# The gate's two VectorE operations at the ends of their units, and a pair of transposes side by side, in the attention loop of an encoder layer

## The chip, the cores and the metric

The kernel runs on one core of one Trainium2 chip. The metric is the device time of one launch in microseconds (us); the median of three runs stands for the kernel. A profile of one execution gives, for each engine, when each instruction ran: TensorE (PE, with its weight loads as PEld), VectorE (DVE), ScalarE (ACT), GpSimd (POOL) and SyncE (SP), which issues most of the transfers.

## The reference, cut to what matters

One encoder layer on two sequences of 512 rows and 1024 columns. An S5 state-space branch and a windowed attention branch (16 query heads, 4 key heads, windows of three blocks of 128) are merged under two gates; an output projection and a squared-ReLU MLP follow.

```python
h = rms_norm(x, ln1)
q, k, v, u, g_att, g_ssm = jnp.split(h @ w_in, IN_SPLITS, axis=-1)
...
s = einsum('nqkgd,njkd->nkgqj', qb, kw) * scale + bias      # banded, masked
p = softmax(concatenate([s, sink_col], -1), -1)[..., :-1]
y_att = einsum('nkgqj,njkd->nqkgd', p, vw)
...
y_ssm = y * sigmoid(y @ w_glu + b_glu)
mixed = sigmoid(g_att) * y_att + sigmoid(g_ssm) * y_ssm
x = x + mixed @ w_out
x = x + square(relu(rms_norm(x, ln2) @ w_up)) @ w_down
```

The change concerns `sigmoid(g_att) * y_att` (the gate's product), the softmax's division, which the kernel does on the finished head outputs, and the transposes of `p`.

## The kernel before, in words

Nearly every product of two matrices is made of three: each operand is split into a rounded high part (a copy on ScalarE) and the remainder, the low part (a subtraction on VectorE or GpSimd).

**The attention loop** (lines 1026 to 1131) runs over eight steps, one for each key head `j` and sequence `sq`. A step has four units, one for each block of 128 queries (`qb`, 0 to 3). A unit handles four heads against two key blocks (at the ends of the sequence) or three. The engines' order inside the loop is written out by hand for TensorE, ScalarE, VectorE and GpSimd (line 1026); SP is not in that list, and its order is the planner's.

Three units are in flight at any time. For the unit `cur`, TensorE computes the scores (`scores`, line 860, two `sps` banks in turn), VectorE adds the bias and takes the maximum (`largest`, line 866), ScalarE takes the exponential (`exp`). For the unit before, `prev`, TensorE transposes `p` block by block (`turn`, line 877, two `tps` banks in turn), ScalarE copies the high part (`high`), VectorE the low part (`low`), and TensorE multiplies by the values into the single bank `po` (`value`, line 892). ScalarE then copies the lower half of `po` (`lower_part`). For the unit before that, `owed`, VectorE adds the two halves into `ya` (`add`, line 902), which empties `po`; the first `value` of `prev` waits for it. Between all this, `project` feeds TensorE with the query projection of the next step (in step 7, which has no next step, with GLU products by `glu_pull`), followed by `square`, `power` (a sum of squares on VectorE and a power on GpSimd), `norm`, and the query's own `turn`, `high` and `low`.

**The gate and the division** of step i come during step i + 1, in the object `late` (class `Divide`, line 908). In block 1 the sums are inverted, transposed and sent through DRAM to be spread over the partitions (`fac`, line 931); the gate's tile is loaded (`load_gate`, line 934). In block 2 `gated` (line 939) multiplies `ya` by the gate. In block 3 `multiply` (line 943) multiplies `ya` by `fac` and stores the result to `mix_scr`. `fac` and the gate's tile take turns in the two buffers of the pool `evp`, tag `ev`. The bias tiles of the next key head are loaded by SP at the end of block 3 of every second step (line 1130).

**The tail** (lines 1132 to 1161) finishes the last unit, with GLU products between the transposes, and starts the merge. `load_gates` (line 688) loads `gs` and `at` (the finished attention from `mix_scr`) for one column of the merge, on GpSimd's queue; `at` uses the pool `evp`, tag `ev` as well. `lower` is the low part of the last piece of GLU weights, on GpSimd. `gated_states`, `mixed` and `parts_of` are the merge itself, mostly on VectorE.

Of the kernel before, what the change touches and what calls it, by code (L numbers as in the profile page):

```python
# [63 lines left out]
def hybrid_layer(ctx, tc, x, rel, onehot, w_qkv, w_ug, vectors, lam, coefs, w_glu, w_out, ln2,  # L64
# [15 lines left out]
    def acc():  # L80
        return ps_acc.tile([P, 512], F32, tag="acc", name="acc")
# [606 lines left out]
    def load_gates(m):  # L688
        tiles = [p.tile([P, NTOK], F32, tag=tag, name=name) for p, tag, name in
                 ((wq, "c_hi", "ga"), (wq, "c_lo", "gs"), (evp, "ev", "at"))]  # L690
        glu_in[m] = tiles
        for t_, scr in zip(tiles[1:], (gs_scr, mix_scr)):
            GP.dma_start(t_, scr[m])
# [32 lines left out]
    def mixed(u):  # L726
        m, s, (ga, gs, at) = sides(u)
        V.tensor_mul(ga, ga, gs)
        V.tensor_add(ga, ga, at)
# [6 lines left out]
    with tc.tile_pool(name="att", bufs=2, reuse_waits="tile") as ap, tc.tile_pool(name="attc", bufs=1, reuse_waits="tile") as ac:  # L736
# [63 lines left out]
        class Tile:  # L800
# [6 lines left out]
            def project(self, n):  # L807
                (j, sq), col = self.key, self.t * P
                for i in range(self.k, min(self.k + n, 3 * KT)):
                    k, p = divmod(i, 3)  # L810
                    hi, lo = weights[j][k // 4]
                    act, w = [(0, hi), (0, lo), (1, hi)][p]
                    PE.matmul(self.ps, hT[sq][act][:, k, col:col + P], w[:, k % 4, :], start=i == 0, stop=i == 3 * KT - 1)  # L813
                self.k += n
# [134 lines left out]
        def load_y(m):  # L949
            if m % 4 == 0:  # L950
                yT.append([q.rearrange("p (m s) k -> p m (s k)", s=2) for q in slot((slot_b, slot_a)[m // 4])])
            for e in range(2):
                SP.dma_start(yT[-1][e][:, m % 4, :].bitcast(F32), y2_scr[e, m * 8:(m + 1) * 8].rearrange("g c t k -> (g c) (t k)"))
# [15 lines left out]
        def glu_pull(n):  # L969
            for _ in itertools.islice(early, n):  # L970
                pass
# [39 lines left out]
        def pieces_of(i):  # L1011

            if i == 0:
                return weight_pieces(1)
            if i == 6:
                return glu_pieces(0, wq, GP)
            if i == 7:
                return glu_pieces(1, cpool, GP) + glu_pieces(2, cpool, GP)
            if i % 2 == 1:
                pending[:] = weight_pieces(i // 2 + 2) if i // 2 + 2 < N_KV else []  # L1020
                return pending[:2]
            return pending[2:]

        pending = []
        prev = owed = lower = None
        with tc.manual_schedule(engines={ET.PE, ET.Activation, ET.DVE, ET.Pool}):
            for i, (j, sq) in enumerate(steps):
                nxt = steps[i + 1] if i + 1 < len(steps) else None
                sums = small.tile([P, G, NB], F32, tag="sm", name="sm", bufs=2)
                ya = ap.tile([P, 2, HALF], F32, tag="ya", name="ya")  # L1030
                extra = pieces_of(i)
                for qb in range(NB):
                    if 1 <= i < 5:
                        e, t = divmod((i - 1) * NB + qb, T)
                        GP.dma_start(y2_scr[e, :, :, t, :].rearrange("g c k -> c g k"), y_scr[e, t])
                    for m in {6: (qb,), 7: ((4, 5), (6,), (7,), ())[qb]}.get(i, ()):
                        load_y(m)
                    cur = Unit(j, sq, qb, sums, ya)
                    n3 = prev.nkb if prev else 0
                    div = Divide(*steps[i - 1], *done) if qb == 1 and i > 0 else None  # L1040
                    new = Tile(*nxt, qb) if nxt else None
                    project = new.project if new else lambda n: glu_pull(n // 2)
                    kd = None
                    if rows and not nxt:
                        rows.pt = acc()
                    if rows and not rows.qn:
                        rows.power()
                    cur.scores(0)
                    cur.largest(0)
                    if qb == 2 and late:  # L1050
                        late.gated()
                    if qb == 3 and late:
                        late.multiply()
                    if i == 7 and qb == 3:
                        load_gates(0)
                        final = Divide(j, sq, sums, ya, True)
                        final.load_gate(ap, "p", 3)
                    cur.scores(1)
                    if owed:
                        owed.add()  # L1060
                    cur.largest(1)
                    if n3:
                        prev.turn(0)
                        prev.high(0)
                    project(6)
                    if n3:
                        prev.low(0)
                    cur.exp(0)
                    cur.exp(1)
                    if rows and not rows.qn:  # L1070
                        rows.norm()
                    if qb == 0 and nxt:
                        kd = key_copies(*nxt)
                    if div:
                        div.invert()
                    cur.scores(2)
                    cur.largest(2)
                    if n3:
                        prev.turn(1)
                        prev.high(1)  # L1080
                    project(4)
                    if n3:
                        prev.value(0, 0)
                    project(2)
                    cur.exp(2)
                    cur.scores(3)
                    if lower:
                        lower()
                        lower = None
                    if n3:  # L1090
                        prev.low(1)
                        prev.value(0, 1)
                    cur.largest(3)
                    if rows:
                        rows.turn()
                    if n3 > 2:
                        prev.turn(2)
                    if kd:
                        key_turn(*nxt, kd)
                    if div:  # L1100
                        div.turn()
                    project(4)
                    if rows:
                        rows.high()
                        rows.low()
                    if n3 > 2:
                        prev.high(2)
                    if n3:
                        prev.value(1, 0)
                    cur.exp(3)  # L1110
                    if n3 > 2:
                        prev.low(2)
                    project(4)
                    if n3:
                        prev.value(1, 1)
                    project(4)
                    if n3 > 2:
                        prev.value(2, 0)
                        prev.value(2, 1)
                    if new:  # L1120
                        new.square()
                    if n3:
                        prev.lower_part()
                    if extra:
                        lower = extra.pop(0)()
                    if qb == 1:
                        late = div
                    owed, prev, rows = prev, cur, new
                    if nxt and qb == NB - 1 and sq == 1:
                        load_biases(nxt[0])  # L1130
                done = sums, ya
            owed.add()
            glu_pull(6)
            for k in range(prev.nkb):
                prev.turn(k)
                prev.high(k)
                prev.low(k)
                glu_pull(4)
            lower()
            gate_out(0)  # L1140
            for k in range(prev.nkb):
                prev.value(k, 0)
                prev.value(k, 1)
            load_gates(1)
            prev.lower_part()
            prev.add()
            glu_pull(10)
            gate_out(1)
            final.invert()
            final.turn()  # L1150
            glu_pull(24)
            final.gated()
            for u in range(2):
                gated_states(u, ap, "qn")
                mixed(u)
            gate_out(2)
            gate_out(3)
            gated_states(2, ap, "qn")
            column_half(3, 0)
            column_half(3, 1)  # L1160
            final.multiply()
# [429 lines left out]
```

## Time and profile before

| | us |
|---|---|
| median of three runs | 1502.4 |
| lowest and highest of them | 1500.92, 1504.12 |
| the profiled execution | 1503.71 |
| its span, first to last instruction | 1501.9 |
| TensorE busy in it | 1453.4 |
| VectorE busy in it | 1106.8 |
| attention loop, from the first score product to the last exponential's unit | about 459.9 to 695 |

The span is that of the instructions; the execution's own time is 1.8 us longer. An entry of the timeline gives the start in us from the span's start, the length, the engine, the line of the kernel, the operation with its output and inputs, and in brackets how long the engine had been idle and what released it. The granted clock of TensorE is 0.998 of full speed over the span. Ends of matrix products are modelled in the profile, so a TensorE that is shown busy may still be short of its best rate.

### The profile page before, as it was taken

Reading aid. Unit: us, or ns where it says so; the run is one execution under the profiler, and the core shown is the slowest. Engines: PE = TensorE matmul, PEld = TensorE weight load, DVE = VectorE, ACT = ScalarE, POOL = GpSimd, SP = SyncE. Lnnn points to the kernel's source line nnn. Section 1 sums busy time; section 2 is a strip of 40 time slices with the busy share of each in tenths; the row PEclk is TensorE's granted clock in tenths of the full one; section 3 lists DMA queues with packets and bytes.
Section 4 is the critical chain, followed back from the end, with each engine's and each line's share of the span. In section 5 each row is a group of like instructions: output and inputs, shape, how many; then the busy total and the mean of one; then the engine's idle time right before and its main releaser. Section 6 shows DMA issues by size and latency. Waiting matters only on the chain.

```text
span 1501.9 us, 22138 instructions
## 1 busy us (share of the span) xinstructions
PE 1453.4 (97%) x8074; PEld 1230.0 (82%) x8074; DVE 1106.8 (74%) x1989; ACT 761.7 (51%) x1362; POOL 212.6 (14%) x372
## 2 busy tenths in 40 slices
PE   6999999999999999999999989999999999999998
PEld 4888888888999888887787868888888888888787
DVE  7998859976646888887975478777777588575653
ACT  6777852235536777775334254445555443433332
POOL 3133341002232443222100000000000000000000
PEclk9999999999999999999999999999999999999999
DMA  4455469229731445275544234444443794454441
GB/s 174 140 169 168 160 208 345 107 100 344 287 132 36 155 135 183 88 252 170 185 135 162 92 115 159 155 154 154 155 154 126 267 352 132 153 182 154 126 123 60
DMA packets 103165, 249.69 MB, mean 166 GB/s; under 512 B 12266, under 2 KB 23786, under 8 KB 103056
## 3 DMA queue, kind: packets, MB, share of 16 engines
q1 hardware_dynamic: 60528, 140.07, 28.7%
q0 software_dynamic: 16896, 53.53, 10.3%
q10 hardware_dynamic: 25632, 54.67, 9.7%
q8 instruction: 64, 1.05, 0.3%
q14 instruction: 45, 0.37, 0.1%
HBM read 173.74 MB, written 90.21 MB: 176 GB/s over the span
## 4 chain that ended last, share of the span: by engine, by line
PE 78%; DVE 8%; ACT 4%; DMA 4%; issue 3%; POOL 1%; ACTq 0%; SPq 0%; DVEq 0%; POOLq 0%
PE acc L185 14%; PE bank L117 13%; PE bank L118 13%; PE bank L116 13%; PE acc L813 4%; PE acc L123 3%; PE acc L117 2%; PE acc L118 2%; PE acc L116 2%; PE sps L547 2%; PE po L896 2%; PE sps L864 1%; PE tps L880 1%; PE sps L645 1%; DMA fac<-rs_scr 1%
## 5 line engine op out<-in xcount | busy, mean ns | idle before, releaser
L185 PE MATMUL acc<-act,c_hi 128*128 128x512 f32 x768 | 249.6, 400 | 1.0 <-DVE act L304 1.0
L117 PE MATMUL bank<-b_lo,a_hi 128*128 128x512 f32 x448 | 174.6, 390 | 1.6 <-DVE b_lo L1460 1.6
L118 PE MATMUL bank<-b_hi,a_lo 128*128 128x512 f32 x448 | 174.3, 389 | 0.0
L116 PE MATMUL bank<-b_hi,a_hi 128*128 128x512 f32 x448 | 173.5, 389 | 0.0
L185 PEld LDWEIGHTS acc<-act,c_hi 128*128 128x128 f32 x768 | 142.2, 189 | 29.1 <-DVE act L304 2.4
L185 PE MATMUL acc<-act,c_lo 128*128 128x512 f32 x384 | 152.5, 397 | 0.0
L1459 ACT CAST a_hi<-d_a 128x1024 fp32r<-128x1024 f32 x56 | 59.0, 1054 | 179.7 <-PE bank L117 176.4
L116 PE MATMUL bank<-act,act 128*128 128x512 f32 x368 | 144.1, 391 | 4.9 <-ACT act L1349 4.9
L117 PE MATMUL bank<-act,act 128*128 128x512 f32 x368 | 143.7, 391 | 0.0
L118 PE MATMUL bank<-act,act 128*128 128x512 f32 x368 | 143.7, 391 | 0.0
L1460 DVE TENSOR_TENSOR a_lo<-d_a,a_hi 128x1024 fp32r<-128x1024 f32 x56 | 68.5, 1224 | 99.9 <-ACT a_hi L1459 99.9
L813 PE MATMUL acc<-w_hi,act 128*128 128x256 f32 x512 | 116.2, 295 | 0.0
L117 PEld LDWEIGHTS bank<-b_lo,a_hi 128*128 128x128 f32 x448 | 84.1, 188 | 20.1 <-DVE b_lo L1460 2.6
L116 PEld LDWEIGHTS bank<-b_hi,a_hi 128*128 128x128 f32 x448 | 84.1, 188 | 17.5
L118 PEld LDWEIGHTS bank<-b_hi,a_lo 128*128 128x128 f32 x448 | 84.1, 188 | 17.3
L813 PEld LDWEIGHTS acc<-w_hi,act 128*128 128x128 f32 x512 | 87.0, 189 | 3.7
L874 ACT ACTIVATE p<-p,nmx 128x257 f32<-128x257 f32 (+1 forms) x128 | 72.1, 563 | 31.2 <-DVE nmx L868 30.2
L116 PEld LDWEIGHTS bank<-act,act 128*128 128x128 f32 x368 | 69.4, 189 | 19.7 <-ACT act L1349 5.3
L123 PE MATMUL acc<-act,gc_hi 128*128 128x512 f32 x256 | 82.6, 401 | 1.8 <-ACT gc_hi L683 1.8
L185 PEld LDWEIGHTS acc<-act,c_lo 128*128 128x128 f32 x384 | 72.4, 189 | 14.0 <-DVE c_lo L176 0.5
L118 PEld LDWEIGHTS bank<-act,act 128*128 128x128 f32 x368 | 69.4, 189 | 14.9 <-DVE act L1350 0.4
L117 PEld LDWEIGHTS bank<-act,act 128*128 128x128 f32 x368 | 69.5, 189 | 14.3
(328 smaller groups left out, 3434.4 us busy)
## 6 DMA issues: line engine op xcount, KB each, us to landing
d_a<-a_scr SPq DMA_DIRECT2D x56, 512.0 KB, 3.6
u_raw<-in_w_up_dram SPq DMA_DIRECT2D x32, 512.0 KB, 5.1
a_scr<-t ACTq DMA_DIRECT2D x64, 256.0 KB, 4.8
k<-in_w_down_dram SPq DMA_DIRECT2D x32, 512.0 KB, 6.4
c_raw<-in_w_ug_dram SPq DMA_DIRECT2D x48, 256.0 KB, 3.7
a_scr<-a ACTq DMA_DIRECT2D x46, 256.0 KB, 2.1
ct_scr<-ctab POOLq DMA_DIRECT2D x16, 576.0 KB, 3.7
ctab_in<-ct_scr POOLq DMA_DIRECT2D x16, 576.0 KB, 7.6
```

The costliest lines, as they stand in the source:

```text
L116: PE.matmul(ps, a[0], b[0], start=first, stop=False)
L117: PE.matmul(ps, a[0], b[1], start=False, stop=False)
L118: PE.matmul(ps, a[1], b[0], start=False, stop=last)
L123: PE.matmul(ps, w[wi][:, k, :], rows[yi], start=k + p == 0, stop=k == KT - 1 and p == 2)
L185: PE.matmul(ps, w[wi][:, k, :], hT[s][hi][:, k, :], start=n == 0, stop=n == 3 * KT - 1)
L547: PE.matmul(ps[:, i * P:(i + 1) * P], bm[:, ri, g, :], u_sb[:, gp * SH + g, :], start=True, stop=True)
L645: PE.matmul(o, ctab[:, g0 % SI + g, ri, 0:T * CH], st[:, ri, g].rearrange("p s k -> p (s k)"), start=False, stop=ri == 1)
L813: PE.matmul(self.ps, hT[sq][act][:, k, col:col + P], w[:, k % 4, :], start=i == 0, stop=i == 3 * KT - 1)
L874: S.activation(p, p, AF.Exp, bias=self.nmx[:, h:h + 1], scale=-1.0, accum_out=self.sums[:, h, self.qb:self.qb + 1])
L896: PE.matmul(self.po, vv, self.hl[i][part], start=i + part == 0, stop=i == self.nkb - 1 and part == 1)
L1459: S.copy(hi, src)
L1460: V.tensor_sub(lo, src, hi.bitcast(F32))
```

## The change

Four edits in the order written out by hand; no operation is added or taken away.

- `gated` leaves its place between the first and the second maximum of block 2, and is written behind the query projection's `square`, ahead of `lower_part`, at the end of the same block.
- `multiply` moves in the same way inside block 3, in steps 1 to 6. With it goes its store on SP.
- In step 7, `multiply` and `load_gates(0)` leave block 3 and stand in the tail, behind the last unit's transposes, high and low parts, and ahead of `lower` and `gate_out(0)`.
- The second block's four transposes, `prev.turn(1)`, move from behind the third head's scores to directly behind the first block's. Their copy, `prev.high(1)`, stays.

```diff
                     cur.scores(0)
                     cur.largest(0)
-                    if qb == 2 and late:
-                        late.gated()
-                    if qb == 3 and late:
-                        late.multiply()
                     if i == 7 and qb == 3:
-                        load_gates(0)
                         final = Divide(j, sq, sums, ya, True)
                         final.load_gate(ap, "p", 3)
                     cur.scores(1)
...
                     cur.largest(1)
                     if n3:
                         prev.turn(0)
+                        prev.turn(1)
                         prev.high(0)
                     project(6)
...
                     cur.scores(2)
                     cur.largest(2)
                     if n3:
-                        prev.turn(1)
                         prev.high(1)
                     project(4)
...
                     if new:
                         new.square()
+                    if qb == 2 and late:
+                        late.gated()
+                    if qb == 3 and late and nxt:
+                        late.multiply()
                     if n3:
                         prev.lower_part()
...
                 prev.high(k)
                 prev.low(k)
                 glu_pull(4)
+            late.multiply()
+            load_gates(0)
             lower()
             gate_out(0)
```

## The prediction

> **What bounds the kernel now.** I read the page's engine line first, then windows cut at the first score product of each unit (one query block of one step), then the timelines of VectorE and TensorE inside those windows, then the chain of waits. Steps are numbered 0 to 7, blocks 0 to 3; times are us.
>
> ```profile
> PE 1453.4 (97%) x8074; PEld 1230.0 (82%) x8074; DVE 1106.8 (74%) x1989; ACT 761.7 (51%) x1362; POOL 212.6 (14%) x372
> ```
>
> TensorE is busy 97% of the span, so an edit on another engine counts only where TensorE waits. The windows show where that is. In order: step 0 blocks 2 and 3 (no gate work there), step 1 blocks 2 and 3, step 2 block 0, step 4 block 3. Columns: length, then busy time (count) of TensorE, its weight loads, VectorE, ScalarE, GpSimd; clock; DMA share and GB/s.
>
> ```profile
> 471.68:479.41 7.73, 7.70 (x57) 7.01 (x56) 6.51 (x17) 6.61 (x16) 2.67 (x4) 1.00 0.12 37
> 479.41:486.34 6.93, 6.93 (x56) 6.61 (x55) 5.77 (x16) 5.69 (x15) 3.54 (x5) 1.00 0.32 91
> 499.48:508.35 8.87, 8.33 (x56) 7.07 (x55) 7.97 (x19) 6.63 (x17) 3.63 (x5) 1.00 0.62 196
> 508.35:516.14 7.79, 7.67 (x56) 6.72 (x54) 6.83 (x18) 5.28 (x14) 2.27 (x4) 1.00 0.88 293
> 516.14:522.64 6.50, 6.50 (x53) 6.26 (x52) 5.39 (x16) 5.05 (x13) 2.85 (x5) 1.00 0.35 118
> 597.67:606.38 8.71, 7.65 (x55) 6.72 (x54) 6.89 (x18) 5.28 (x14) 1.43 (x3) 1.00 0.40 141
> ```
>
> Step 0 does the same matrix work without a gate: block 2 takes 7.73 there and 8.87 in step 1, block 3 takes 6.93 and 7.79. VectorE's timeline, a piece of the chain of waits, and TensorE's timeline (steps 1 and 7) say why.
>
> ```profile
> 501.03 1.23 DVE L941 TENSOR_TENSOR ya<-ya,gate 128x1024 f32<-128x1024 f32 x1
> 502.18 0.84 DVE L906 TENSOR_TENSOR ya<-po,ol 64x256 f32<-64x256 f32 x2
> ```
> ```profile
> 501.11 1.15 DVE ya L941
> ```
> ```profile
> 503.16 0.47 PE L896 MATMUL po<-ph,va 128*128 128x512 f32 x1 [0.39 <-DVE ya L906]
> ...
> 682.23 0.47 PE L896 MATMUL po<-ph,va 128*128 128x512 f32 x1 [1.00 <-DVE ya L906]
> ...
> 691.21 0.47 PE L896 MATMUL po<-ph,va 128*128 128x512 f32 x1 [1.80 <-DVE ya L906]
> ```
>
> The first value product needs the one `po` bank, which VectorE's `add` (L906) empties. The gate's product (L941) stands ahead of that `add` and lies on the chain with its full 1.15 (its row says 1.23; what follows starts 0.08 before its end). In block 3 the division (L945, 1.22 to 1.23, so some 1.14 on a chain) stands at the same place. That is the wait the change removes; the count of operations stays.
>
> **The change, part by part.**
>
> *Product out of block 2 (steps 1 to 6).* Step 0's block 2 has the same number of TensorE entries but one and the same ScalarE time (6.61 against 6.63), so I take its length: 8.87 - 7.73 = 1.14 less, six times.
>
> *Division out of block 3.* By step 0, 7.79 - 6.93 = 0.86. It delayed VectorE by 1.14 and cost 0.86, so a block forgives 1.14 - 0.86 = 0.28 of lateness at this place and passes the rest to TensorE.
>
> *The same operations at the ends of their blocks.* They now stand between the last low part and the next unit's sum of squares and first maximum. Step 0, end of block 2:
>
> ```profile
> 478.32 0.69 DVE L889 TENSOR_TENSOR pl<-tps,ph 128x512 fp32r<-128x512 f32 x1
> 479.26 0.42 DVE L823 TENSOR_REDUCE ms<-sq 128x4 f32<-128x256 f32 x1 [0.24 <-ACT sq L819]
> 479.84 0.48 DVE L868 CUSTOM_DVE_ANT_0 p<-sps,bias,vec 128x256 f32<-128x256 f32 x1 [0.16 <-PE sps L864]
> ```
>
> VectorE is free at 479.01. The product would end 1.15 later, at 480.16, and the sum of squares (0.42, less the same 0.08) lets the maximum start at 480.50 instead of 479.84: 0.66 late, of which 0.28 is forgiven. So block 3 pays 0.38 and takes 7.31 (bounds: 0, if idle time later in the block takes it up, and the whole 0.66). The division at the end of block 3 does the same to block 0 of the next step, which has no row with such a delay: it has 6.50 - 5.39 = 1.11 of VectorE idle time, about what block 3 of step 0 has (6.93 - 5.77 = 1.16), so I take 0.38 again, with the same bounds. Queued behind the moved operation on VectorE stand the sum of squares, and through it GpSimd's power and the query norm; the norm comes on VectorE only behind both first maxima and a low part, so these are late by no more than the rest.
>
> Per step: -1.14 - 0.86 + 0.38 + 0.38 = -1.24. Six steps: **-7.4**.
>
> *A transfer that was waited for.* The division in steps 4 and 7:
>
> ```profile
> 599.44 1.22 DVE L945 TENSOR_TENSOR ya<-ya,fac 128x1024 f32<-128x1024 f32 x1 [0.84 <-DMA fac<-rs_scr]
> ...
> 689.08 1.23 DVE L945 TENSOR_TENSOR ya<-ya,fac 128x1024 f32<-128x1024 f32 x1 [1.67 <-DMA fac<-rs_scr]
> ```
>
> At the end of the block `fac` has landed. Step 4's block 3 was 8.71 against 7.79 in step 1: **-0.9** beyond the above (0 if that late landing belongs to one execution). In step 7, which has no next unit, the product leaves block 2 and the division leaves the loop: TensorE's waits of 1.00 and 1.80 go, **-2.8**; without the transfer's 1.67 it would be 1.13.
>
> *Second transposes ahead.* The same four transposes, the same count; their evacuation keeps its place on ScalarE and VectorE. The `tps` bank they need is read for the last time by the last low part of the unit before, which that unit's last value product already waits for (after a unit with a key turn or a division's turn, by their evacuation, which comes sooner), so no new wait comes. TensorE gets those four transposes of work between the first and the second pair of scores, which covers a late first maximum, but not the `add` or the first low part, whose work ahead on TensorE is unchanged. I count **0** (bounds -0.3 and +0.3 in all, by the 0.28 that a block forgives).
>
> *The tail.* The last division goes behind the last low part; behind it GpSimd's loads for the first merge, because `at` takes the buffer of `fac`.
>
> ```profile
> 699.30 0.69 DVE L889 TENSOR_TENSOR pl<-tps,ph 128x512 fp32r<-128x512 f32 x1 [0.67 <-ACT ph L884]
> 701.91 0.85 DVE L906 TENSOR_TENSOR ya<-po,ol 64x256 f32<-64x256 f32 x2 [1.92 <-ACT ol L900]
> ...
> 706.70 0.69 DVE L729 TENSOR_TENSOR ga<-ga,at 128x512 f32<-128x512 f32 x1
> ```
> ```profile
> 696.71 1.29 POOL L684 TENSOR_TENSOR gc_lo<-c_raw,gc_hi 128x512 fp32r<-128x512 f32 x1 [7.54 <-ACT gc_hi L683]
> 697.94 0.56 POOL L693 DMA_DIRECT2D gs<-gs_scr  x1
> ```
> ```profile
> DMA to landing us min/median/max: 4.6/5.0/8.3
> ```
>
> In the clock of before, the division runs from 699.99 to 701.13, inside the 1.92 of idle time: free, and if that cover were gone it would cost its 1.14. `at` is then issued at 701.13 and lands 4.6 to 8.3 later (the landing line is that of `at`), at 705.7 to 709.4; the merge reads it at 706.70. The wait is 0 to 2.7. With the store of the division and GpSimd's next two loads in flight I take about the middle, **+1.3**. VectorE runs almost without a break behind it, so this is passed on. On GpSimd the last glu weight part (696.71) and the next `gs` (697.94) come behind `at`, some 5 later; the product of column 2 and the second half's merge, which read them, come behind 24 more early products and the first merge. On SP the stores move past bias and weight loads (a rival below).
>
> Sum: -7.4 - 0.9 - 2.8 + 1.3 = **-9.8**. The profiled execution took 1503.71 with a span of 1501.9, so 1.8 lie around the span, which nothing here touches; its span would become 1492.1. The median of the runs shown is 1502.4, 1.3 below that execution, and the forecast is made from it: 1502.4 - 9.8 = **1492.6**.
>
> **The rivals.**
>
> *All hidden.* The late start costs blocks 3 and 0 nothing: 12 x 0.38 = 4.6 more gained, 1488.0; without the tail's 1.3, 1486.7. For it: over 1.1 of VectorE idle time per block. Against: it lies late in the block, the `add` early. Chance 0.12.
>
> *SP's queue.* SP's order here is the planner's. If it leaves the division's store ahead of the bias loads, these wait for the division, in steps 1, 3 and 5.
>
> ```profile
> 509.31 0.32 SPq L780 DMA_DIRECT2D bias<-line_scr  x1
> 510.45 0.37 SPq L946 DMA_DIRECT2D mix_scr<-ya  x1
> 511.73 2.66 SPq L780 DMA_DIRECT2D bias<-line_scr  x3
> ```
> ```profile
> DMA to landing us min/median/max: 2.3/4.6/7.2
> ```
>
> With block 3 at 7.31, block 0 would begin at 508.35 + 7.31 = 515.66, the division end about 0.8 later and the next bias load go out near 517, landing (last line, of the bias loads) at 519 to 524. Its maximum is the third of block 0, at about half of the 6.50, near 519: 0 to 5 lost, so some 2.5 x 3 = 7.5, 1500.1. For it: the store is written ahead of the loads. Against: one such load, though written later, already stands ahead of the store, so the planner goes by readiness. Chance 0.10.
>
> *VectorE is the bound.* If the delay passes on whole, -1.14 - 0.86 + 1.15 + 1.14 = +0.29 a step: 1502.4 + 1.7 - 0.9 - 2.8 + 1.3 = 1501.7, no change. For it: 7.97 busy of 8.87. Against: step 1's block 3 and step 2's block 0 hold only 6.83 and 5.39. Chance 0.09.
>
> *Slower: GpSimd holds the moved operation up.* One product of before overlapped a GpSimd operation of 128x512; GpSimd's rows stand first, VectorE's behind:
>
> ```profile
> 500.98 1.04 POOL L826 TENSOR_TENSOR rq<-ms,neg_half 128x4 f32<-128x4 f32 x1
> ...
> 508.60 0.23 POOL L825 TENSOR_SCALAR ms<-ms 128x4 f32<-128x4 f32 x1 [4.20 <-DVE ms L823]
> ...
> 678.95 1.29 POOL L684 TENSOR_TENSOR gc_lo<-c_raw,gc_hi 128x512 fp32r<-128x512 f32 x1 [4.67 <-ACT gc_hi L683]
> ```
> ```profile
> 679.06 2.26 DVE L941 TENSOR_TENSOR ya<-ya,gate 128x1024 f32<-128x1024 f32 x1
> ```
>
> It took 2.26 instead of 1.23, 1.03 more. At the 14 new places (7 products, 7 divisions) that is 14.4, 1507.0. It turns the sign from 9.8 / 14 = 0.70 a place on. Against it: ahead of the sum of squares GpSimd idles (4.20 there), and just there the operations go. Chance 0.04. [...]
>
> **How the numbers follow.** Forecast 0.62, the rivals 0.12, 0.10, 0.09 and 0.04, the rest (0.03) unnamed. The range goes from all hidden, 1486.7, past the forecast with both late starts paid in full and the tail at 2.7 (12 x 0.28 + 1.4 = 4.8 more, 1497.4) to the lower part of SP's rival, about 1498.5. A measurement tells 0.2%, 3.0, from no change, so faster means below 1499.4: the forecast, all hidden, half of SP's rival and some of the unnamed, 0.81. Within 0.2%: the rest of SP's rival and the bound on VectorE, 0.14. Slower: 0.05.
>
> **What would show it.** Block 2 near 7.7, block 3 near 7.3, block 0 near 6.9; the first value product of a unit no longer released by L906; no idle time of L945 before `fac`; L729 waiting 0 to 2.7 for `at`. Wrong would be: blocks 3 and 0 longer by over 0.7 each, a maximum released by a bias transfer, L941 or L945 above 1.3, TensorE waiting at the second transposes.

## The result, and the profile after

The changed kernel takes **1487.0 us** (median of four runs, 1485.79 to 1488.63) against 1503.3 for the kernel before beside it (1500.92 to 1507.67): a ratio of 0.9891, 95% interval 0.9878 to 0.9904. The profiled execution's span is 1486.0 against 1501.9, 15.9 less, where 9.8 had been predicted. The direction and the main mechanism came as predicted; the gain was larger than the sum.

The engine line of the changed kernel's page. TensorE's busy time fell by 6.4 and the span by 15.9, with the same 8074 products, so 9.5 of it was waiting as the profile counts it. What the 6.4 is made of the profile does not tell apart.

```profile
PE 1447.0 (97%) x8074; PEld 1230.8 (83%) x8074; DVE 1102.7 (74%) x1989; ACT 761.0 (51%) x1362; POOL 209.8 (14%) x372
```

The changed kernel's windows, cut at the first score product of each unit: step 1 blocks 2 and 3, step 2 block 0, step 4 block 3, step 7 block 2; then step 7 block 3, which ends here at the first GLU product behind its last value product, and 15 us of the merge. The columns are those of the prediction's windows.

```profile
500.17:507.90 7.73, 7.71 (x57) 7.06 (x55) 6.99 (x18) 6.65 (x17) 3.54 (x5) 1.00 0.59 179
507.90:515.09 7.19, 7.19 (x55) 6.62 (x54) 6.87 (x18) 5.28 (x14) 2.27 (x4) 1.00 0.90 275
515.09:521.63 6.54, 6.54 (x54) 6.26 (x52) 5.99 (x17) 5.05 (x13) 2.84 (x5) 1.00 0.60 215
592.10:599.30 7.20, 7.20 (x55) 6.63 (x54) 6.88 (x18) 5.27 (x14) 1.42 (x3) 1.00 0.34 114
667.64:674.51 6.87, 6.87 (x39) 6.01 (x38) 5.79 (x14) 5.13 (x13) 1.41 (x2) 1.00 0.75 222
674.51:680.96 6.45, 6.45 (x40) 5.61 (x39) 4.90 (x14) 4.74 (x13) 2.45 (x3) 1.00 0.69 233
...
719.70:734.70 15.00, 13.40 (x58) 10.46 (x57) 14.53 (x22) 6.23 (x11) 1.63 (x4) 1.00 0.51 170
```

The same stretches of step 7 and of the merge in the kernel before:

```profile
677.97:686.49 8.52, 7.52 (x40) 5.80 (x38) 7.14 (x14) 5.12 (x13) 3.58 (x4) 1.00 0.65 191
686.49:695.32 8.83, 6.93 (x39) 5.53 (x38) 5.74 (x14) 4.98 (x13) 1.29 (x1) 1.00 0.58 205
...
734.00:749.00 15.00, 13.40 (x51) 10.24 (x50) 13.64 (x20) 6.11 (x10) 1.08 (x2) 0.89 0.54 174
```

In each of these windows of the loop after, TensorE's busy time is within 0.02 of the length: the waits that the profile shows are gone. Block 2 went from 8.87 to 7.73, block 3 from 7.79 to 7.19, block 0 from 6.50 to 6.54. Step 4's block 3, which had waited for `fac`, went from 8.71 to 7.20; step 7's two blocks from 8.52 and 8.83 to 6.87 and 6.45.

From the loop's start to step 7's block 3 that makes 6 x 1.14 + 5 x 0.60 + 1.51 - 6 x 0.04 + 1.65 = 12.8; with 0.4 from step 0, which the run with the transposes alone explains below, 13.2. The traces have 226.6 before and 213.5 after, 13.1 less. Step 7's block 3 gives 2.4.

Two differences are put down to the clock and not to the edit. The loop started 1.1 later than before (460.97 against 459.86): ahead of it the changed kernel's execution had 3.4 us of halved clock from 329.4 on, where before had none.

```profile
326.00:336.00 10.00, 8.19 (x44) 7.20 (x43) 3.13 (x6) 6.60 (x11) 0.53 (x1) 0.83 0.22 78
```

So at the first entry of the merge 14.3 are left (719.07 against 704.75). In the merge it is the other way round: before ran at a mean granted clock of 0.89 over 15 us and after at 1.00, which is 0.11 x 15 = 1.65. The gain of the edit in these two traces is therefore about 15.9 + 1.1 - 1.6 = 15.4.

### The profile page after: what moved, and what is told of

Same layout as the page of the kernel before. It is cut to its first block, busy times and chain, and to the rows that moved or that the text cites. A ratio compares the mean times of both kernels' runs of the same rounds, so it can differ in the third digit from the quotient of the medians.

```text
span 1486.0 us, 22128 instructions
## 1 busy us (share of the span) xinstructions
PE 1447.0 (97%) x8074; PEld 1230.8 (83%) x8074; DVE 1102.7 (74%) x1989; ACT 761.0 (51%) x1362; POOL 209.8 (14%) x372
## 4 chain that ended last, share of the span: by engine, by line
PE 84%; DVE 6%; ACT 4%; DMA 3%; issue 3%; POOL 1%; ACTq 0%; SPq 0%; DVEq 0%; POOLq 0%
PE acc L185 14%; PE bank L117 13%; PE bank L118 13%; PE bank L116 13%; PE acc L813 6%; PE acc L123 4%; PE po L896 3%; PE sps L864 2%; PE tps L880 2%; PE acc L117 2%; PE acc L118 2%; PE acc L116 2%; PE sps L547 2%; PE acc L835 1%; DMA toep<-toep_scr 1%
## 5 line engine op out<-in xcount | busy, mean ns | idle before, releaser
L117 PEld LDWEIGHTS bank<-act,act 128*128 128x128 f32 x368 | 69.5, 189 | 14.3
```

The source lines that it names most:

```text
L117: PE.matmul(ps, a[0], b[1], start=False, stop=False)
```

## The experiments

Every kernel below is timed against the kernel before on the same chip. "Changed kernel" means the one with all four edits. Times by block are from windows cut as above.

**The gate's product alone.** Against the kernel before:

```diff
                     cur.largest(0)
-                    if qb == 2 and late:
-                        late.gated()
                     if qb == 3 and late:
                         late.multiply()
...
                         new.square()
+                    if qb == 2 and late:
+                        late.gated()
                     if n3:
                         prev.lower_part()
```

> Gate's product alone moved to the end of block 2. Theory (what counts is how late VectorE reaches the add of a unit): block 2 falls from 8.87 to 7.7 in steps 1 to 6, but in block 3 the late start (0.55) and the division (1.14), which is still ahead of the add, come together; with about 0.35 forgiven, block 3 grows from 7.79 to about 8.3. Together -1.14 + 0.5 a step, -3.9 in six steps, step 7 some -1.6: about 5 us faster than before (ratio 0.9965). Rival (each moved operation has its own price, whatever the other does): block 3 stays within 0.2 of 7.79, about 8 us faster (0.9945).

The kernel took 1501.8 against 1503.4, a ratio of 0.9987 (0.9976 to 0.9999). Its windows of step 1, blocks 2 and 3:

```profile
499.57:507.28 7.71, 7.67 (x56) 6.99 (x55) 6.95 (x18) 6.65 (x17) 3.54 (x5) 1.00 0.59 184
507.28:515.62 8.34, 7.67 (x56) 6.71 (x54) 7.67 (x19) 5.28 (x14) 3.27 (x4) 1.00 0.83 269
```

Block 2 has its 1.15, and block 3 gives back 0.55 of it: the late start is paid in full when the division still stands in the same block. The rival, which had both parts at prices of their own, fell. The expected time was missed, though: the loop was 6.3 shorter than before, yet the time only 1.6, where about 5 had been expected. From step 7's block 3 on this profile lost 2.6 against before. In step 7 the division still stands early and waits for `fac`, and the value product behind it waits 1.74; a stretch of halved clock follows at 686.7, in which the product of 0.40 takes 0.63. VectorE's timeline:

```profile
682.76 1.32 DVE L945 TENSOR_TENSOR ya<-ya,fac 128x1024 f32<-128x1024 f32 x1 [1.51 <-DMA fac<-rs_scr]
```

**The division alone**, with its move into the tail; the gate's product stays early:

```diff
                     if qb == 2 and late:
                         late.gated()
-                    if qb == 3 and late:
-                        late.multiply()
...
+                    if qb == 3 and late and nxt:
+                        late.multiply()
                     if n3:
                         prev.lower_part()
...
+            late.multiply()
+            load_gates(0)
             lower()
```

> Division alone moved (end of block 3, tail in step 7, with the loads of the first merge); the gate's product stays in the middle of block 2. Theory: block 2 stays at 8.87, block 3 falls to 6.95 (nothing late ahead of it), block 0 is 6.54; -0.82 x 6 = -4.9, the wait for fac in step 4 -0.9, step 7 -2.4: about 8 us faster (ratio 0.9945). With the gate alone this adds up to about 13, less than the 16 of both together, because the gate's gain in block 2 is only kept when the division has left block 3. Rival (own prices): the two add up to what both bring together.

The kernel took 1495.2 against 1503.4, a ratio of 0.9949 (0.9933 to 0.9965). Step 1, blocks 2 and 3, and step 2, block 0:

```profile
498.69:507.56 8.87, 8.31 (x56) 7.05 (x55) 8.01 (x19) 6.66 (x17) 3.64 (x5) 1.00 0.62 180
507.56:514.51 6.95, 6.95 (x55) 6.63 (x54) 6.06 (x17) 5.27 (x14) 2.27 (x4) 1.00 0.86 286
514.51:521.03 6.52, 6.52 (x54) 6.24 (x52) 5.96 (x17) 5.17 (x14) 2.84 (x5) 1.00 0.52 183
```

Block 3 falls to 6.95, the length of step 0's, and block 0 pays 0.02. One half gave 1.6, the other 8.2, both together 16.2. Part of the difference lies in the loops (6.3 and 5.7 less than before, against 13.1 with both), because block 3 forgives lateness only once. Without a delay it takes 6.95. A late start of 0.55 costs 0.24 there (7.19), the division's 1.14 costs 0.84 (7.79), the two together 1.39 (8.34): each time the lateness less about 0.3. The larger part lies in the first half alone. The division's 8.2 is what its trace has: 5.7 in the loop and 2.4 in step 7's block 3 (6.43 against 8.83). The gate's half has 6.3 in its loop but kept the early division in step 7, where its block 3 took 10.36; of the 4.7 by which its time falls short of its loop, 1.5 are that block. Where the rest went is not shown.

**The transposes alone, and the changed kernel without them.**

```diff
                         prev.turn(0)
+                        prev.turn(1)
                         prev.high(0)
...
-                        prev.turn(1)
                         prev.high(1)
```

> Second block's transposes alone moved, gate and division as before. Theory: nothing of what TensorE waits for changes, blocks 2 and 3 stay 8.87 and 7.79, ratio 1.000 within 0.0005 (0.7 us). Rival (the wait for the late first maximum counts): up to 0.3 a block in blocks 2 and 3, 12 x 0.3 = 3.6 us faster (0.9976).

> The changed kernel with the second block's transposes put back behind the third head's scores. Theory (the idle time of VectorE within the block takes up the late start): same as the changed kernel within 1 us, ratio to before 0.989 to 0.990, blocks 3 and 0 at 7.2 and 6.55. Rival (the transposes ahead are what hides the late first maximum): blocks 3 and 0 each 0.3 longer, 7.5 and 6.8, 3.6 us lost of the gain, ratio 0.9915.

Alone, the edit left the time at 1503.3, a ratio of 0.9999 (0.9988 to 1.001), with blocks 2 and 3 at 8.88 and 7.79 as before. Undone in the changed kernel it gave 1488.0, a ratio of 0.9899 (0.9881 to 0.9917), with blocks of 7.72, 7.19 and 6.54 as in the changed kernel. In the time the edit can't be told from no change. One block shows it, in every profile that has it: block 1 of step 0 falls from 7.12 to 6.68, and with the edit undone it is 7.12 again. The kernel before, its wait in that block from TensorE's timeline, and the kernel with the transposes alone:

```profile
464.57:471.68 7.11, 6.76 (x50) 6.23 (x49) 6.13 (x15) 5.86 (x16) 2.67 (x4) 1.00 0.12 36
```
```profile
466.93 0.44 PE L864 MATMUL sps<-kh,qa 128*128 128x384 f32 x1 [0.35 <-DVE nmx L868]
```
```profile
464.08:470.76 6.68, 6.68 (x51) 6.28 (x50) 6.13 (x15) 5.78 (x16) 2.66 (x4) 1.00 0.09 28
```

There the first maximum starts 1.69 into the block, the scores that need its bank waited 0.35 for it, and with the transposes ahead of them that wait is gone. Where the moved operations put the first maximum, 0.99 into blocks 3 and 0, the transposes gain nothing: those blocks are the same with the edit undone.

The run with the transposes alone showed something else: its waits for `fac` fell on steps 1, 4 and 7, against 4 and 7 before. VectorE's timeline, step 1:

```profile
509.21 1.22 DVE L945 TENSOR_TENSOR ya<-ya,fac 128x1024 f32<-128x1024 f32 x1 [0.85 <-DMA fac<-rs_scr]
```

So the 0.9 is no fixed price of step 4, which waited 0.84 before, 0.46 here and not at all with the gate's product alone. One to three such waits came with each profiled execution that has the division early in all steps.

**The changed kernel once more**, for the spread between sets of runs:

> The changed kernel once more, beside the next one on the same chip, and to see which blocks wait for fac in another execution. Ratio to before 0.989; blocks 2, 3, 0 at 7.72, 7.19, 6.54; no wait for fac anywhere, since the division now comes some 5 us after its landing.

It took 1487.0 against 1502.1, a ratio of 0.9897 (0.988 to 0.9913), with blocks of 7.73, 7.18 and 6.55.

**More lateness.** In four places of the changed kernel VectorE does a superfluous product on the gate's tile behind the moved operation: half a tile at the ends of step 2 block 2 and step 3 block 3, a whole one at the ends of step 4 block 2 and step 5 block 3.

```diff
                     if qb == 3 and late and nxt:
                         late.multiply()
+                    if (i, qb) in ((2, 2), (4, 2), (3, 3), (5, 3)):
+                        n = 1 if i in (2, 3) else 2
+                        V.tensor_mul(late.ga[:, 0:n], late.ga[:, 0:n], late.ga[:, 0:n])
```

> The changed kernel with a superfluous product on VectorE (the gate's tile, no longer needed, times itself) behind the moved one: half length (about 0.6) at the end of block 2 in step 2 and of block 3 in step 3, full length (1.15) at the end of block 2 in step 4 and of block 3 in step 5. Theory (a block forgives a fixed lateness and passes the rest on; by the gate alone, 1.69 late cost 1.37 in block 3, so 0.32 forgiven; block 0 forgives 0.5): block 3 of steps 2 and 4 at 7.8 and 8.3, block 0 of steps 4 and 6 at 7.1 and 7.7, others unchanged. Rival (the block's idle time on VectorE takes it up, 0.3 in block 3 and 0.55 in block 0 being left): block 3 grows by 0.3 and 0.85, block 0 by 0.05 and 0.6.

Windows of the blocks that follow the four places (step 2 block 3, step 4 block 0, step 4 block 3, step 6 block 0):

```profile
535.49:543.42 7.93, 7.80 (x56) 6.75 (x54) 7.58 (x19) 5.38 (x14) 2.30 (x4) 1.00 0.61 195
...
571.48:578.62 7.14, 7.04 (x54) 6.41 (x52) 6.59 (x18) 5.14 (x13) 2.84 (x5) 1.00 0.74 212
592.96:601.40 8.44, 7.79 (x55) 6.77 (x54) 8.08 (x19) 5.38 (x14) 1.42 (x3) 1.00 0.30 108
...
629.49:637.16 7.67, 7.15 (x53) 6.42 (x52) 7.12 (x18) 5.14 (x13) 1.96 (x4) 1.00 0.91 303
```

The half tile makes the first maximum 0.74 later (537.21 in a block that starts at 535.49, against 508.88 and 507.90), and block 3 is 7.93 - 7.19 = 0.74 longer: every further bit is passed on. The whole tile makes it 1.25 later and costs block 3 1.25. Block 0 starts its first maximum 0.60 and 1.13 later and pays 0.60 and 1.13. So what a block forgives is a fixed allowance, some 0.3 in block 3 and some 0.5 in block 0, and the change uses it up in both. The rival, that idle time of VectorE in the block would take up a part of the further delay, fell. (One time of 1494.8 was taken, 7.8 above the changed kernel, of which the blocks explain 3.7; that execution's mean granted clock is 0.995 against 0.998, and a stretch of halved clock lies in its merge, near 727.4.)

**Another place.** Both operations go directly behind the unit's last maximum instead of behind `square`:

```diff
                     cur.largest(3)
+                    if qb == 2 and late:
+                        late.gated()
+                    if qb == 3 and late and nxt:
+                        late.multiply()
                     if rows:
                         rows.turn()
```

> Both operations at a third place: behind the fourth head's maximum, ahead of the query's low part and the last low part, all else as in the changed kernel. Theory: the next unit no longer starts late, but the last low part comes later, for which the last value product waits already: block 2 at 7.72 + 0.93 = 8.6 (VectorE idles 0.2 there), block 3 at about 7.3 (it idles 0.5 there), block 0 at 6.50; 6 us slower than the changed kernel, near 1493. Rival (any place behind the add is as good): within 1 us of the changed kernel.

The kernel took 1497.2 in one run, 10 above the changed kernel. Its window of step 1's block 2, and the last value product in it from TensorE's timeline:

```profile
499.89:508.58 8.69, 7.70 (x57) 7.05 (x55) 8.05 (x19) 6.66 (x17) 3.54 (x5) 1.00 0.70 205
```
```profile
508.24 0.50 PE L896 MATMUL po<-pl,va 128*128 128x512 f32 x1 [0.99 <-DVE pl L889]
```

Here the product delays the last low part (L889), and the unit's last value product waits 0.99 for that: block 2 pays 0.96 against the changed kernel and block 3 0.39, 8.1 over six steps, which is what the loop lost (221.66 against 213.54). Block 3's share was expected smaller (7.3, not 7.58), and why it is larger is not shown. "Away from the `add`" is not enough: the place has to be one at which VectorE owes TensorE nothing soon.

**Off VectorE.** The two operations of steps 1 to 6 go to GpSimd, in the middle of the same units; the tail's division stays on VectorE.

```diff
                     if lower:
                         lower()
                         lower = None
+                    if qb == 2 and late:
+                        late.gated(GP)
+                    if qb == 3 and late and nxt:
+                        late.multiply(GP)
```

> Gate's product and division of the loop taken off VectorE: GpSimd does them in the middle of blocks 2 and 3, where it idles some 4 us (step 7's last division stays in the tail on VectorE). Theory: no late start is left, block 3 falls from 7.19 to 6.95 and block 0 from 6.54 to 6.50, block 2 stays: -0.28 x 6 = -1.7, some 1485.3, ratio to before 0.988. Rival (the two engines shut each other out, as at 679.06 of the kernel before): VectorE's operations of two SBUF inputs grow, or GpSimd's power comes late and the query norm waits: a block longer by up to 1, so slower than the changed kernel by 3 us or more.

The kernel took 1487.1, a ratio of 0.9897 (0.9882 to 0.9912). GpSimd's timeline:

```profile
501.25 2.40 POOL L941 TENSOR_TENSOR ya<-ya,gate 128x1024 f32<-128x1024 f32 x1
...
506.87 2.40 POOL L945 TENSOR_TENSOR ya<-ya,fac 128x1024 f32<-128x1024 f32 x1
```

Its windows of step 1 block 3 and step 2 block 0:

```profile
505.19:512.15 6.96, 6.96 (x55) 6.64 (x54) 5.75 (x16) 5.28 (x14) 4.64 (x5) 1.00 0.94 311
512.15:518.65 6.50, 6.50 (x54) 6.26 (x52) 5.34 (x16) 5.18 (x14) 2.85 (x5) 1.00 0.71 232
```

Both blocks fall to what they are without any gate work, which confirms that 0.24 and 0.04 is all that the late starts still cost; the loop is 1.5 shorter than the changed kernel's (212.05 against 213.54). In the time this isn't seen: the medians are equal, and the profile lost 2.8 behind the loop, with a halved clock in the merge at 719.8 (the product of 0.39 takes 0.63 from 720.04 on). It is no clear improvement.

**Step 7's division and loads back** at the start of its block 3, all else as changed; run twice, the second time with more executions.

```diff
                     if i == 7 and qb == 3:
+                        late.multiply()
+                        load_gates(0)
                         final = Divide(j, sq, sums, ya, True)
...
-            late.multiply()
-            load_gates(0)
             lower()
```

> The changed kernel with step 7's division and the loads of the first merge put back at the start of its block 3; steps 1 to 6 as changed. Theory (in step 7 the loss was the late fac and GpSimd's hold on block 2's product, not the place as such): steps 1 to 6 unchanged; fac lands about 674.7 in the changed kernel, 0.7 ahead of that place, so block 3 waits for it 0 to 0.5, and the add comes at 2.9 behind the block's start, just when the first value product wants it: block 3 of step 7 at most 0.5 longer than 6.45, the merge behind it as before, within 1 us of the changed kernel in all. Rival (the place costs its full length there as in the other steps): block 3 of step 7 longer by 1.1 to 2, 1488 to 1489.

> The same edit as in the run with step 7's division at the start of its block 3, timed in more rounds, since that run's interval was wide. Theory (the place of step 7's division costs a wait for fac, because a shortened block 2 brings block 3 ahead of fac's landing, and often a halved clock behind the wait): above the changed kernel again, 1489 to 1495, ratio 0.991 to 0.995, L945 in step 7 waiting 1 to 2 for fac. Rival (that run was disturbed): within 1 of the changed kernel, near 1487.5, ratio 0.990.

The two sets gave 1494.3, a ratio of 0.9914 (0.9884 to 0.9944), and 1491.2, a ratio of 0.9928 (0.9914 to 0.9943). The first expectation, that this would cost less than 1, failed. VectorE's timeline of the first profile, and TensorE's:

```profile
677.49 1.24 DVE L945 TENSOR_TENSOR ya<-ya,fac 128x1024 f32<-128x1024 f32 x1 [1.59 <-DMA fac<-rs_scr]
```
```profile
679.64 0.47 PE L896 MATMUL po<-ph,va 128*128 128x512 f32 x1 [1.75 <-DVE ya L906]
...
682.94 0.63 PE L123 MATMUL acc<-act,gc_lo 128*128 128x512 f32 x1
```

The shorter block 2 brings the division to 675.9, while the second half of `fac` lands at 677.4; from 681.2 the clock is halved (the product of 0.39 takes 0.63, and the mean from 674.97 to 683.10 is 0.88). That block took 10.37 instead of 6.44. In the second profile `fac` had landed (L945 at 674.00 with no wait) and the clock was whole, and the block was still 0.6 longer than the changed kernel's:

```profile
673.16:680.22 7.06, 6.91 (x39) 5.52 (x38) 6.04 (x15) 4.98 (x13) 2.39 (x2) 1.00 0.82 282
```

That execution took 1489.5, within the 1489.1 to 1493.6 of its set. So of the second expectation the time holds and the wait does not: a wait for `fac` is shown for one of two profiles only. The loss itself is likely but not firm. The first set's interval takes in the changed kernel's ratios of 0.9891 and 0.9897, the second set's begins where that of the changed kernel's second set ends, and the changed kernel was not timed beside either. What the other executions lost is not shown.

**Step 7's division at the end of its block 3**, as in the other steps; the loads stay in the tail.

```diff
-                    if qb == 3 and late and nxt:
+                    if qb == 3 and late:
                         late.multiply()
...
-            late.multiply()
             load_gates(0)
```

> Step 7's division at the end of its block 3, where steps 1 to 6 have it, instead of in the tail; the loads for the merge stay in the tail. Theory (what counts in step 7 is that the division stands behind fac's landing and behind the add of its unit, not that it is in the tail): as the changed kernel, 1486.5 to 1488.5, ratio 0.990, L945 without a wait for fac, block 3 of step 7 within 0.2 of 6.45. Rival (only the tail is free, since every other place delays the last unit): 1 to 2 slower, the division's 1.14 passed to the first value product of the tail.

The kernel took 1489.6, a ratio of 0.9913 (0.9898 to 0.9927). Its window of step 7's block 3, and VectorE's timeline:

```profile
674.92:681.36 6.44, 6.44 (x39) 5.61 (x38) 5.65 (x15) 4.74 (x13) 2.45 (x3) 1.00 0.65 233
```
```profile
680.53 1.22 DVE L945 TENSOR_TENSOR ya<-ya,fac 128x1024 f32<-128x1024 f32 x1
682.18 0.85 DVE L906 TENSOR_TENSOR ya<-po,ol 64x256 f32<-64x256 f32 x2 [0.43 <-ACT ol L900]
```

By the trace the theory held: no wait for `fac`, a block as long as the changed kernel's, the division inside idle time of the `add` (which still waits 0.43 for ScalarE), and a loop of 213.55. The rival's delay in the tail is not there. The time is nevertheless 2.6 above the changed kernel's, somewhat more than the rival's 1 to 2, in sets whose intervals overlap a little; the 2.5 by which the two profiles' spans differ lie ahead of the loop (0.4) and from 772 on, behind the merge (the rest). Whether the place has to do with that is open.

## Why the prediction held, and where its sum was off

The forecast of 1492.6 was 5.6 above the measured 1487.0, which lies 0.3 above the low end of the range. That end was the rival *All hidden* and not a term of the forecast, so that the time fell into the range owes something to luck. The direction and the wait that was removed do not.

*Product out of block 2:* -1.14 predicted, 8.87 to 7.73 measured in every step from 1 to 6. Right, and in the reason too: by the view of line 896, the value products of the changed kernel wait only for the low parts (L889, 4.2 in all, 14 times), never for L906.

*Division out of block 3:* -0.86 predicted, -0.84 measured where it was moved alone.

*The same operations at the ends of their blocks:* the step was right in kind and **mis-sized**. VectorE's timeline of the changed kernel at the end of step 1's block 2, and in the tail:

```profile
507.42 1.22 DVE L941 TENSOR_TENSOR ya<-ya,gate 128x1024 f32<-128x1024 f32 x1
508.55 0.41 DVE L823 TENSOR_REDUCE ms<-sq 128x4 f32<-128x256 f32 x1
508.88 0.48 DVE L868 CUSTOM_DVE_ANT_0 p<-sps,bias,vec 128x256 f32<-128x256 f32 x1
...
685.57 1.22 DVE L945 TENSOR_TENSOR ya<-ya,fac 128x1024 f32<-128x1024 f32 x1
687.57 0.85 DVE L906 TENSOR_TENSOR ya<-po,ol 64x256 f32<-64x256 f32 x2 [0.78 <-ACT ol L900]
...
692.35 0.69 DVE L729 TENSOR_TENSOR ga<-ga,at 128x512 f32<-128x512 f32 x1
```

The first maximum starts 0.98 into block 3 (508.88 after 507.90) against 0.43 in step 0 of before: 0.55 late, not 0.66. The product starts 0.08 before the low part ends, an overlap that the sum left out at this one place, and the rows behind it overlap by another 0.03. Block 3 pays 0.24 of it, where 0.38 had been put. In block 0 the maximum is 0.55 late as well (0.99 into the block against 0.44), and it pays 0.04: there the step failed that carried block 3's 0.28 over to block 0 because the two have about the same idle time. Its allowance is some 0.5. Idle time in a block says little about the lateness that it forgives; what makes up the allowance was not tried. The two terms cost 0.28 a step, not 0.76: 2.9 of the missing gain.

*Wait for a transfer:* step 4's 0.9 went, though such waits differ in step and size from execution to execution. In the changed kernel L945 waits for `fac` nowhere.

*Step 7:* -2.8 predicted, -1.65 and -2.38 measured. The sum took only TensorE's waits ahead of the first value product. In block 2 it also lost weight the row of 2.26 that the text used for its GpSimd rival: at its new place the product takes 1.22.

```profile
673.68 1.22 DVE L941 TENSOR_TENSOR ya<-ya,gate 128x1024 f32<-128x1024 f32 x1
```

The blocks were 1.0 and 1.9 short of their length by waits (8.52 against 7.52 busy, 8.83 against 6.93), and busy time fell as well, by 0.65 and 0.48; what that is made of the runs do not show. Of the two, the division's place is tested: back at the start of block 3 with its loads, it makes the block 0.6 and 3.9 longer in the two profiles. The times are 4.2 and 7.3 above the changed kernel's, with the reservations said there.

*Second transposes:* 0 predicted, with bounds of 0.3 either way. Measured is nothing in the blocks with the moved operations, and 0.45 less in step 0's block 1, of which block 3 of that step gives back some 0.04. The reason given, that the transposes cover a late first maximum, is right; the sum did not look for a block where it is late enough.

*The tail:* **this step failed**: +1.3 was predicted, 0 measured. It said that `at` takes the buffer of `fac`, so that its load waits for the division. GpSimd's timeline of the changed kernel, and of the kernel before:

```profile
677.79 0.56 POOL L693 DMA_DIRECT2D at<-mix_scr  x1
...
687.08 0.55 POOL L693 DMA_DIRECT2D at<-mix_scr  x1 [2.95 <-DVE ya L945]
```
```profile
681.97 0.56 POOL L693 DMA_DIRECT2D at<-mix_scr  x1
```

The first `at` goes out 7.8 ahead of the division, lands at 682.8 and is read at 692.35 (L729, above) without a wait. As the pool has two buffers (line 137) and `fac` still held one, this `at` has the other, the gate's, which the product of block 2 had freed at 674.9. Only the second `at` gets `fac`'s: it waits 2.95 for the division, lands at 691.9 and is late for nobody. The trace of before had shown this already: there the first `at` went out at 681.97, and the division that reads `fac` began at 689.08. The code does not show it, since it asks for `fac`'s buffer ahead of the gate's (lines 925 and 928), and taking turns in that order would have given the first `at` the buffer of `fac`. By the loads' own order (gate at 649.05, `fac` at 669.79, then the two `at`) the buffers do take turns; that this order decides is not shown. The division itself ran inside idle time, as predicted.

Of the 6.1 between 9.8 and the 15.9 in the profile, the late starts make 2.9, the tail 1.3, step 7 1.2, the transposes 0.4 and the clock 0.5 (1.6 in the merge less 1.1 ahead of the loop). Together these are 6.3, 0.2 too much.

The rivals. *All hidden* (1486.7 to 1488.0) has the time but not the whole mechanism: block 3 still pays 0.24. *SP's queue* fell: SP's timeline has the bias loads of step 1 ahead of the store.

```profile
509.39 3.94 SPq L780 DMA_DIRECT2D bias<-line_scr  x4
515.86 0.37 SPq L946 DMA_DIRECT2D mix_scr<-ya  x1
```

*VectorE as the bound* fell with blocks 3 and 0. *GpSimd in the way* fell too; the view of tile `ya` in the changed kernel gives the shortest, the median and the longest of both operations in ns:

```profile
L941 DVE TENSOR_TENSOR ya<-ya,gate x8: 1160/1215/1216, 507.4 to 688.6; 128x1024 f32<-128x1024 f32 x8
L945 DVE TENSOR_TENSOR ya<-ya,fac x8: 1212/1216/1219, 514.6 to 699.3; 128x1024 f32<-128x1024 f32 x8
```

None is stretched: at the end of step 1's block 2, for example, GpSimd is idle from 504.99 to 509.06. In before, the product of 2.26 started at 679.06 beside GpSimd's operation of 678.95, and GpSimd's copy behind that one (L856, at 680.18) took 1.19, where the median of its 32 is 0.20; in the changed kernel the longest of them takes 0.20. In the run with both operations on GpSimd, VectorE's 16 operations of step 1's block 3 take 5.75 in all beside GpSimd's product of 2.40, against 5.77 for 16 in step 0 of before: in sum they did not grow.

## What to carry to other kernels

An operation that nobody waits for soon belongs where its engine next owes the critical engine the least: three places of the same product here gave blocks of 8.87, 8.69 and 7.73. Price the lateness that it leaves behind by an allowance for each block, measured with a dummy operation of known length, and never count an allowance twice; two edits that draw on one allowance have to be tried together. Before saying whose buffer a load will wait for, look in the trace at hand for when it went out: a load that was issued while a tile was still to be read does not have that tile's buffer.

## What was not expected of the hardware

The granted clock of TensorE falls to half for 3.4 us at places that differ between executions of one program, some of them behind short waits. Before had such a stretch in the merge at 738.1 (from 738.5 to 741.5 the clock is 0.50, and the product of 0.39 takes 0.63), after had none there; TensorE's timeline of before has four waits there, 0.61, 0.73, 1.23 and 0.36 within some 7 us, that of after 0.80, 0.73, 0.75 and 0.85. Ahead of the loop it was the other way round: both have a wait of 1.81, ending at 329.04 in after and at 328.61 in before, and only after has the stretch, from 329.4 on. Of eleven profiles beside before (all but that of the transposes alone), eight have a stretch that begins between 716 and 735, in the merge; in before it cost 1.65 by the mean clock. In the run with step 7's division put back a stretch began at 681.2, behind a wait of 1.75 that ended at 679.64; in before a wait of 1.80 at the same place brought none. This sets the limit on what can be told here: behind the loop the profiles of programs that are equal there differ by as much as 2.8 (the run on GpSimd against the changed kernel).

Stretches of 3.4 also begin at 878.9 in the changed kernel and at 895.1 in before, each at the end of a wait of 4.91; those in the merge, at 329.4 and at 681.2 follow waits of 1.8 at most. What sets a stretch off is not shown.
